# First loads by single k-tiles, small parameters behind them, h transposed before its modulation, raw weights in idle attention tiles

## The chip, the cores and the metric

The kernel runs on one core of one Trainium2 chip. The metric is the device time of one execution in microseconds (us), the median of several; lower is better. The core has five engines that run side by side: TensorE (PE, matmuls and transposes), VectorE (DVE), ScalarE (ACT), GpSimd (POOL) and SyncE (SP, which here only issues DMAs). Data go from HBM to SBUF by DMA, and matmuls write to PSUM, of which the kernel uses eight banks of 128 x 512 floats.

## The reference

Two layers; 256 tokens, width 1024. All values are float32.

```python
def hybrid_layer(x, c, ...):
    mod = silu(c) @ w_ada + b_ada                       # 1024 x 3072
    shift, scale, gate = split(mod, 3)
    h = rms_norm(x, norm_g) * (1 + scale) + shift
    z = h @ w_in                                        # 1024 x 2976
    c_q, c_kv, k_rope, g_mla, q_b, k_b, v_b, g_moba = split(z)
    o_mla = mla_attention(c_q, c_kv, k_rope, positions, ...)
    o_moba = moba_attention(q_b, k_b, v_b, ...)
    y = concat([silu(g_mla) * o_mla, silu(g_moba) * o_moba]) @ w_out
    return x + gate * y
```

With 256 tokens MoBA has a single block, so both attentions are causal attentions with 8 heads, MLA with low-rank q and kv (`w_uq`, `w_ukv`) and rotary keys, MoBA with a relative bias.

## The kernel before

**Precision by splitting.** A weight piece is 256 rows of a weight matrix (two k-tiles of 128) by up to 512 columns, loaded raw as float32. ACT (or DVE) casts it to a rounded high part `whi`, DVE subtracts to get the low part `wlo`, and h is split in the same way. Each product is three matmuls: high by high, high by low, low by high. `plan` lists the pieces in the order of their use: for layer 0 first a, ga, gb for each pair of k-tiles (pieces 0 to 11), then uq, uq, ukv, bq, bk, bv and the output weights. `load_piece` (L540) loads one into a buffer, `splitter` and `split_lo` (L553, L574) split it, the first `HALVES` pieces by single k-tiles.

**The first stage of layer 0.** `w_ada` for shift (w=0) and scale (w=1) is loaded in five rounds of k-tiles (0), (1), (2, 3), (4, 5), (6, 7) by `load_first` (L1315), into tiles that attention needs only later. `sum_first` (L1331) sums each round on PE with silu(c), copies the sums out, transposes them and makes shift and gain of these k-tiles. `first_h` (L1418) and `h_T` (L783) transpose the normalised x, apply gain and shift in PSUM and write h high and low. Then the projections a (tile za), ga (zga) and gb (zgb) run k-tile by k-tile. `loader` (L1427) sets the order of these loads on SP's queue. Sixteen small parameters are loaded from POOL's queue right at the start.

**Behind it** come bq, MLA's q and kv, bk, bv, attention in eight steps, and the output projection y; layer 1 does the same with its own order. `modulation` (L718) loads layer 0's gate and layer 1's shift and scale in blocks of 512 columns and sums each on PE in a gap.

**What sets the order.** Instructions are emitted by a planner at build time. `Clock` (L75) keeps an estimated time for each engine and for the DMA queue (D); generators yield the time or the condition for which they wait, and what is ready by the estimate comes first. `run` (L164) goes through the projections' units, and lets optional work in (`offer`) where PE would wait. The engines execute what was emitted for them in order and wait on semaphores. Numbers such as `SLACK`, `BIAS`, `AHEAD`, `URGENT` and `D_0` change only that order. Until the estimate reaches `DUMMY`, `warm_up` (L1436) puts filler matmuls (tile `warm`) into PE's queue.

Of the kernel before, what the change touches and what calls it, by code (L numbers as in the profile page):

```python
# [11 lines left out]
F32 = mybir.dt.float32  # L12
# [9 lines left out]
D = 1024  # L22
# [9 lines left out]
RAW = 3  # L32
ADA_LAG = 0.25
# [4 lines left out]
DENSE = 0.6  # L38
BQ_FIRST = 2
ON = ("T", "T")  # L40
EARLY = True
FIRST = 0
# [12 lines left out]
AHEAD = 4  # L55
SLACK = 0.35
URGENT = 2
BIAS = 0.7
WARM = 7
D_LAT = 0.95  # L60
D_0 = 4.0
HALVES = 12
# [157 lines left out]
class Metered:  # L220
# [18 lines left out]
    def _cost1(self, op, out, args, kw):  # L239
        if op == "preload_act_table_set":  # L240
            return 1.3
        n = 1
        for d in out.shape[1:]:
            n *= d
        if self._name == "P":
            return 0.06 + n / 510.0
        if self._name == "T":
            lhs = kw["lhsT"] if "lhsT" in kw else args[1]
            mode = lhs.shape[0] <= 64, out.shape[0] if out.shape[0] in (32, 64) else 128
            switch = 0.16 if mode != self.__dict__.get("_mode", mode) else 0.0  # L250
            self._mode = mode
            if "lhsT" not in kw:
                return switch + 0.109
            if lhs.dtype != F32:
                return switch + 0.012 + n / 2400.0
            return switch + {32: 0.01 + n / 2400.0, 64: 0.01 + n / 1200.0}.get(out.shape[0], max(0.218, n / 600.0))
        aps = sum(not isinstance(v, (int, float, str)) for k, v in kw.items() if k in ("scale", "bias"))
        ins = [a for a in list(args[1:]) + [kw.get("in0"), kw.get("in1")] if hasattr(a, "space")]
        psum = PSUM in [a.space for a in ins]
        if self._name == "A":  # L260
            return (0.061 if psum else 0.096) + n / 1200.0 + 0.093 * aps + (0.19 if "accum_out" in kw else 0.0)
        if op == "tensor_reduce":
# [9 lines left out]
def trunk(ctx, tc, x, c, positions, norm_g, w_ada, b_ada, w_in, mla_q_norm_g, mla_w_uq,  # L272
# [32 lines left out]
    nc.sync.dma_start(xs[:, 0], x[0, 0:128, :])  # L305
    nc.sync.dma_start(xs[:, 1], x[0, 128:256, :])
# [7 lines left out]
    G.dma_start(pos_i, positions[0].rearrange("(t p) -> t p", p=128))  # L314
    G.dma_start(flat[:, 0:16], invf.unsqueeze(0))
# [11 lines left out]
    G.dma_start(rows_b[V_QN:V_QN + 4], mla_q_norm_g.rearrange("l (k p) -> (l k) p", p=128))  # L327
    G.dma_start(rows_b[V_KN:V_KN + 2], mla_kv_norm_g)
    G.dma_start(rows_b[V_MQ:V_MQ + 2, 0:64], mla_q_g[:, 0:64])
    G.dma_start(rows_b[V_MK:V_MK + 2, 0:64], mla_k_g[:, 0:64])  # L330
    for i, g in enumerate((mla_q_g, mla_k_g)):
        for l in range(DEPTH):
            c0 = 16 + 32 * (DEPTH * i + l)
            G.dma_start(flat[:, c0:c0 + 32], g[l:l + 1, 64:96])
    for a in (0, 64):
        G.dma_start(rows_b[V_BQ:V_BQ + 2, a:a + 64], moba_q_g)
        G.dma_start(rows_b[V_BK:V_BK + 2, a:a + 64], moba_k_g)
# [4 lines left out]
    G.dma_start(rb_s[0:32], rel_bias)  # L342
    oh_s = sp.tile([33, 384], F32, tag="PT", bufs=PTS, name="oh_s")
    G.dma_start(oh_s, onehot)
# [3 lines left out]
                    base=128, channel_multiplier=1)  # L348

# [162 lines left out]
    def load(dst, src, *keys):  # L512
        nc.sync.dma_start(dst, src)
        n = 128 * 4
        for d in dst.shape[1:]:
            n *= d
        clk.t["D"] = max(clk.t["D"], clk.now + 1.7) + 0.05 + n / (3.6e5 if dst.shape[-1] >= 256 else 2.5e5)
        clk.mark(*keys, at=clk.t["D"] + D_LAT)
# [19 lines left out]
    early = ("raw", "raw", "raw", "ga_hi", "ga_lo", "gate", "vb", "raw", "raw", "raw", "ga_hi", "ga_lo")  # L538

    def load_piece(i):  # L540
        key, a, src = pieces[i]
        tag = early[i] if i < len(early) else "raw"
        yield from take(tag)
        pool_ = {"raw": wp, "vb": sp}.get(tag, cp)
        raw = pool_.tile([128, 2, 512], F32, tag=tag, bufs=RAW if tag == "raw" else 1, name=f"raw_{key[0]}{key[1]}_{a}")
        load(raw[:, :, 0:src.shape[2]], src, ("raw", i))
        halves[key, a] = raw, tag

# [4 lines left out]
    def splitter():  # L553
        for i, (key, a, src) in enumerate(pieces):
            n = src.shape[2]
            yield from until(("raw", i))
# [7 lines left out]
            halves[key, a] = hi, lo  # L564
            for ks in parts(i):
                yield from clk.idle("A", urgent, lambda: held(i))
                copy(hi[:, ks, 0:n], raw[:, ks, 0:n])
            start(split_lo(i, raw, tag), clk.end + clk.LAT)
# [5 lines left out]
    def split_lo(i, raw, tag):  # L574
        key, a, src = pieces[i]
        n = src.shape[2]
        hi, lo = halves[key, a]
        for ks in parts(i):
            yield from clk.idle("V", lambda: i <= used[0] + URGENT, lambda: held(i))
            V.tensor_tensor(lo[:, ks, 0:n], raw[:, ks, 0:n], hi[:, ks, 0:n].bitcast(F32), op=ALU.subtract)  # L580
        give(tag)
        clk.mark(("w", key, a))
# [84 lines left out]
    def on_vector(todo, begin, period):  # L667

        for i, ((m, w, j), k) in enumerate(todo):
# [15 lines left out]
            if k == KT - 2:  # L685
                yield
                start(gate_sums(m, j, acc, ones), clk.now)
# [30 lines left out]
    def modulation(l, period):  # L718

        by_k = lambda blocks: [(b, k) for b in blocks for k in range(0, KT, 2)]  # L720
        gates_ = by_k((l, 2, j) for j in range(2))
        next_ = by_k((l + 1, w, j) for j in range(2) for w in (1, 0)) if l + 1 < DEPTH else []
        start(ada_loader(l, (gates_ + next_)))
        if ON[l] == "V":
            yield clk.now + period[1]
            start(on_vector(gates_, clk.now, period[0]), clk.now)
        start(on_tensor((gates_ if ON[l] == "T" else []) + next_, clk.now + period[1], period[2]), clk.now)
# [102 lines left out]
    def proj_unit(name, l, o, k, t):  # L830
# [11 lines left out]
        return unit((("w", key, k // 2), ("h", l, k, t)), k == 0, emit, key, k // 2)  # L842

    def gate_unit(name, l, o, k, b):
# [14 lines left out]
        return unit((("w", key, k // 2), ("h", l, k, 0), ("h", l, k, 1)), k == 0, emit, key, k // 2)  # L859


    def layer(l):
# [86 lines left out]
        def mla_q(t):  # L949
# [8 lines left out]
            for g in range(2):  # L958
                yield from take("ps")
# [28 lines left out]
        def mla_kv(t):  # L988
# [10 lines left out]
            for g in range(2):  # L999
                yield from take("ps")  # L1000
# [426 lines left out]
    def loader():  # L1427
        order = [(0, 1), (0, 0), 0, (1, 1), (1, 0), 1, 2, (2, 1), (2, 0), 3, 4, (3, 1), (3, 0), 5, 6, (4, 1), (4, 0),
                 *range(7, len(pieces))]
        for what in order:  # L1430
            if isinstance(what, int):
                yield from load_piece(what)
            else:
                yield from load_first(*what)
# [26 lines left out]
    clk.mark(("x", 0), at=4.6)  # L1461
    clk.mark(("x", 1), at=6.2)
# [3 lines left out]
    start(angles(), 30)  # L1466
    start(vectors(), 6.2)
    start(loader(), 0.0)
    for r in range(len(rounds)):
        start(sum_first(r))  # L1470
# [68 lines left out]
```

## Time and profile before

| | |
|---|---|
| time, median of 3 runs | 310.87 us (310.55 to 311.05) |
| the profiled execution, in all | 309.71 us |
| its span | 307.6 us |
| PE busy | 296.6 us (96%) |
| DVE busy | 217.0 us (71%) |
| ACT busy | 211.0 us (69%) |
| POOL busy | 13.6 us (4%) |
| DMA | 65.2 MB, 212 GB/s in the mean |

The span runs from the first to the last instruction of the profile; the time in all has some 2 us more around it. Busy shares are means over stages with different limits. Matmul ends are modelled and overlap with the next matmul, so a busy PE can still lose time between two kinds of matmul. A row "31.89 0.69 DVE L230 ..." starts at 31.89 us and lasts 0.69; L230 is the line through which all metered engines' instructions are issued, so instructions are told apart by their tiles: `out<-in`.

### The profile page before, as it was taken

The numbers are of one execution on the slowest core, as the hardware profiler recorded it, in microseconds if no ns is written. First come the engines' busy times: TensorE is split into PE (matmuls) and PEld (weight loads), VectorE is DVE, ScalarE is ACT, GpSimd is POOL, SyncE is SP. The second block draws the span as 40 slices with busy tenths as digits, with TensorE's granted clock in tenths as the row PEclk, the third lists the DMA queues.
The fourth block names the chain that finished last, engine by engine and source line by source line (L and its number), as shares of the span: only waits on it lengthen the run. The fifth ranks groups of instructions, "written<-read, shape, count | busy, mean of one in ns | idle before, by whom it ended". The sixth has DMA issues, their size and how long they took to land.

```text
span 307.6 us, 5595 instructions
## 1 busy us (share of the span) xinstructions
PE 296.6 (96%) x1976; PEld 234.7 (76%) x1976; DVE 217.0 (71%) x635; ACT 211.0 (69%) x516; POOL 13.6 (4%) x40
## 2 busy tenths in 40 slices
PE   6989999999999899999999998999999999999995
PEld 5757779986668588665775968879999778777884
DVE  1344798664997979784876778699877598857544
ACT  5443367796695886986678896877587959685710
POOL 8700000000010000000000000000000000000000
PEclk9799999999999999999999999999999999999998
DMA  7999996895979975781843976665606450621012
GB/s 237 315 351 355 362 372 193 275 389 204 359 212 376 329 256 172 255 286 25 320 120 122 336 258 215 200 168 175 205 12 208 128 174 32 207 78 57 3 65 71
DMA packets 40299, 65.20 MB, mean 212 GB/s; under 512 B 2685, under 2 KB 16325, under 8 KB 40272
## 3 DMA queue, kind: packets, MB, share of 16 engines
q1 hardware_dynamic: 39360, 63.71, 62.5%
q0 software_dynamic: 816, 1.12, 1.4%
q8 instruction: 15, 0.25, 0.3%
q14 instruction: 12, 0.10, 0.1%
q10 hardware_dynamic: 96, 0.02, 0.0%
HBM read 63.79 MB, written 1.06 MB: 211 GB/s over the span
## 4 chain that ended last, share of the span: by engine, by line
PE 81%; DVE 7%; DMA 5%; ACT 5%; issue 1%; SPq 0%
PE y L230 15%; PE zbv L230 7%; PE ada L230 7%; PE zgb L230 7%; PE zga L230 7%; PE zbq L230 6%; PE zbk L230 6%; PE s L230 6%; PE za L230 4%; PE oT L230 4%; DMA raw_bv<-in_w_in_dram 3%; PE ptr L230 3%; PE q L230 2%; PE qtr L230 2%; DMA ada<-in_w_ada_dram 2%; PE warm L230 1%
## 5 line engine op out<-in xcount | busy, mean ns | idle before, releaser
L230 ACT ACTIVATE P<-P,sm 128x128 f32<-128x128 f32 (+1 forms) x116 | 47.8, 446 | 6.7 <-DVE sm L230 6.6
L230 PE MATMUL ada<-ada,crep 128*32 128x512 f32 (+2 forms) x272 | 25.2, 471 | 1.5 <-DMA ada<-in_w_ada_dram 1.5
L230 PE MATMUL y<-whi_o,gm 128*128 128x512 f32 (+1 forms) x72 | 23.8, 386 | 0.5 <-DVE gm L230 0.5
L230 DVE TENSOR_TENSOR wlo_o<-raw_o,whi_o 128x1024 fp32r<-128x1024 f32 x16 | 19.5, 1222 | 3.8 <-ACT whi_o L230 3.8
L230 PE MATMUL zga<-h_hi,whi_ga 128*128 128x256 f32 x64 | 19.3, 302 | 0.0
L230 PE MATMUL zgb<-h_hi,whi_gb 128*128 128x256 f32 x64 | 19.2, 300 | 0.0
L230 PE MATMUL zga<-h_hi,wlo_ga 128*128 128x256 f32 x64 | 18.2, 285 | 0.7 <-DVE wlo_ga L230 0.7
L230 PE MATMUL zgb<-h_hi,wlo_gb 128*128 128x256 f32 x64 | 18.1, 283 | 0.0
L230 PE MATMUL zga<-h_lo,whi_ga 128*128 128x256 f32 x64 | 18.1, 283 | 0.0
L230 PE MATMUL zgb<-h_lo,whi_gb 128*128 128x256 f32 x64 | 18.1, 283 | 0.0
L230 ACT CAST whi_o<-raw_o 128x1024 fp32r<-128x1024 f32 x15 | 15.6, 1044 | 1.6 <-PE y L230 1.6
L230 PEld LDWEIGHTS y<-whi_o,gm 128*128 128x128 f32 x72 | 13.1, 189 | 3.4 <-DVE gm L230 0.9
L230 PE MATMUL ptr<-ident,P 128*128 128x128 f32 x96 | 15.6, 273 | 0.0
L230 ACT ACTIVATE htr<-htr,ss 128x128 f32<-128x128 f32 (+1 forms) x21 | 9.7, 473 | 8.4 <-PE htr L230 5.0
L230 PEld LDWEIGHTS ptr<-ident,P 128*128 128x128 f32 x96 | 12.1, 140 | 4.4 <-DVE sm L230 0.8
L230 PEld LDWEIGHTS ada<-ada,crep 128*32 128x32 f32 x272 | 6.4, 110 | 11.4 <-issue 8.8
L230 PE MATMUL y<-whi_o,ga_hi 128*128 128x512 f32 (+1 forms) x36 | 15.0, 417 | 0.0
L230 PE MATMUL zbv<-whi_bv,h_hi 128*128 128x512 f32 x32 | 14.3, 446 | 0.0
L230 DVE CUSTOM_DVE_ANT_0 P<-s,bt 128x128 f32<-128x128 f32 (+1 forms) x32 | 9.5, 354 | 6.7 <-PE s L230 6.6
L230 PE MATMUL y<-whi_o,ga_lo 128*128 128x512 f32 (+1 forms) x36 | 13.4, 373 | 0.5 <-DVE ga_lo L230 0.5
L230 PE MATMUL zbk<-whi_bk,h_hi 128*128 128x512 f32 x32 | 13.8, 431 | 0.0
L230 PEld LDWEIGHTS zgb<-h_hi,whi_gb 128*128 128x128 f32 x64 | 12.2, 191 | 2.1 <-issue 2.1
(336 smaller groups left out, 878.5 us busy)
## 6 DMA issues: line engine op xcount, KB each, us to landing
ada<-in_w_ada_dram SPq DMA_DIRECT2D x44, 512.0 KB, 7.8
raw_o<-in_w_out_dram SPq DMA_DIRECT2D x16, 512.0 KB, 3.7
raw_ga<-in_w_in_dram SPq DMA_DIRECT2D x8, 512.0 KB, 6.0
raw_gb<-in_w_in_dram SPq DMA_DIRECT2D x8, 512.0 KB, 6.1
raw_bq<-in_w_in_dram SPq DMA_DIRECT2D x8, 512.0 KB, 3.9
raw_bk<-in_w_in_dram SPq DMA_DIRECT2D x8, 512.0 KB, 4.5
raw_bv<-in_w_in_dram SPq DMA_DIRECT2D x8, 512.0 KB, 4.7
raw_a<-in_w_in_dram SPq DMA_DIRECT2D x8, 416.0 KB, 6.1
```

The source lines that it names most:

```text
L230: r = f(*args, **kw)
```

## The change

- **Loads.** x, then round 0 of `w_ada`, then one k-tile each of pieces 0, 1 and 2 (a, ga, gb), round 1, the other k-tile of each, round 2 and so on as before. The three pieces are loaded by two DMAs each. A k-tile of a piece can be used when that k-tile is split.
- **Small parameters.** The 16 small loads leave POOL's queue at the start and are issued behind a copy that waits for the last load of round 0.
- **h.** For layer 0, `h_T` transposes the normalised x without waiting for shift and gain; these are applied in PSUM as before, once they are there.
- **Raw weights.** Four instead of three raw buffers; pieces 12 to 19 go to `bqT`, `bkT`, `kT`, raw, raw, raw, `ga_hi`, `ga_lo`.
- **Planner.** New numbers and estimates, another order of the `w_ada` blocks behind the first stage, one spare PSUM bank asked for by MLA's q and kv.

```diff
-RAW = 3
-ADA_LAG = 0.25
+RAW = 4
+ADA_LAG = 0.1
-DENSE = 0.6
+DENSE = 0.3
-ON = ("T", "T")
+ON = ("TTTTTT", "TT")
+LOADS = ("x0", "x1", (0, 1), (0, 0))
+LATER = True
+SINGLE = 3
+BEHIND = ("bqT", "bkT", "kT", "raw", "raw", "raw", "ga_hi", "ga_lo")
+QS = 1
+ANGLES = 30
+AFTER_0 = (0, 1, 2)
+AFTER_1 = (0, 1, 2)
-FIRST = 0
+ORDER = (0, 4, 1, 2, 5, 3)
+FIRST = 8
-AHEAD = 4
-SLACK = 0.35
-URGENT = 2
-BIAS = 0.7
+AHEAD = 3
+SLACK = 0.25
+URGENT = 1
+BIAS = 0.65
-D_0 = 4.0
-HALVES = 12
+D_0 = 2.1
+HALVES = 9
...
+            if mode[0]:
+                return switch + max(0.109, n / 1200.0)
...
-    nc.sync.dma_start(xs[:, 0], x[0, 0:128, :])
-    nc.sync.dma_start(xs[:, 1], x[0, 128:256, :])
...
-    G.dma_start(pos_i, positions[0].rearrange("(t p) -> t p", p=128))
-    G.dma_start(flat[:, 0:16], invf.unsqueeze(0))
...
-    G.dma_start(rows_b[V_QN:V_QN + 4], mla_q_norm_g.rearrange("l (k p) -> (l k) p", p=128))
...
+    behind = cp.tile([128, 1], F32, name="behind")
+
+    def small_loads():
+
+        if LATER:
+            yield from until(("first", 0, 0, 1))
+            G.tensor_copy(behind, st[0, 0][-1][:, 0:1])
+        G.dma_start(pos_i, positions[0].rearrange("(t p) -> t p", p=128))
+        G.dma_start(flat[:, 0:16], invf.unsqueeze(0))
+        G.dma_start(rows_b[V_QN:V_QN + 4], mla_q_norm_g.rearrange("l (k p) -> (l k) p", p=128))
...
+        G.dma_start(rb_s[0:32], rel_bias)
+        G.dma_start(oh_s, onehot)
+        return
+        yield
...
-        clk.t["D"] = max(clk.t["D"], clk.now + 1.7) + 0.05 + n / (3.6e5 if dst.shape[-1] >= 256 else 2.5e5)
+        clk.t["D"] = max(clk.t["D"], clk.now + 1.7) + 0.02 + n / (3.6e5 if dst.shape[-1] >= 256 else 2.9e5)
...
-    early = ("raw", "raw", "raw", "ga_hi", "ga_lo", "gate", "vb", "raw", "raw", "raw", "ga_hi", "ga_lo")
+    early = ("raw", "raw", "raw", "ga_hi", "ga_lo", "gate", "vb", "raw", "raw", "raw", "ga_hi", "ga_lo", *BEHIND)
 
     def load_piece(i):
         key, a, src = pieces[i]
         tag = early[i] if i < len(early) else "raw"
         yield from take(tag)
-        pool_ = {"raw": wp, "vb": sp}.get(tag, cp)
+        pool_ = {"raw": wp, "ga_hi": cp, "ga_lo": cp, "gate": cp}.get(tag, sp)
         raw = pool_.tile([128, 2, 512], F32, tag=tag, bufs=RAW if tag == "raw" else 1, name=f"raw_{key[0]}{key[1]}_{a}")
-        load(raw[:, :, 0:src.shape[2]], src, ("raw", i))
         halves[key, a] = raw, tag
+        if i < SINGLE:
+            for k in range(2):
+                load(raw[:, k:k + 1, 0:src.shape[2]], src[:, k:k + 1], ("raw", i, k))
+                yield
+        else:
+            load(raw[:, :, 0:src.shape[2]], src, ("raw", i, 0), ("raw", i, 1))
 
 
     def held(i):
@@ -553,7 +577,7 @@
     def splitter():
         for i, (key, a, src) in enumerate(pieces):
             n = src.shape[2]
-            yield from until(("raw", i))
+            yield from until(("raw", i, 0))
             if i > used[0] + AHEAD:
                 yield lambda: i <= used[0] + AHEAD
             yield from take("w")
@@ -562,10 +586,12 @@
             nm = f"{key[0]}{key[1]}_{a}"
             hi, lo = (wp.tile([128, 2, 512], F32R, tag=t_, bufs=SPLITS, name=f"{t_}_{nm}") for t_ in ("whi", "wlo"))
             halves[key, a] = hi, lo
+            start(split_lo(i, raw, tag), clk.now)
             for ks in parts(i):
+                yield from until(("raw", i, ks.start))
                 yield from clk.idle("A", urgent, lambda: held(i))
                 copy(hi[:, ks, 0:n], raw[:, ks, 0:n])
-            start(split_lo(i, raw, tag), clk.end + clk.LAT)
+                clk.mark(("hi", i, ks.start))
             yield
 
     def parts(i):
@@ -576,8 +602,10 @@
         n = src.shape[2]
         hi, lo = halves[key, a]
         for ks in parts(i):
+            yield from until(("hi", i, ks.start))
             yield from clk.idle("V", lambda: i <= used[0] + URGENT, lambda: held(i))
             V.tensor_tensor(lo[:, ks, 0:n], raw[:, ks, 0:n], hi[:, ks, 0:n].bitcast(F32), op=ALU.subtract)
+            clk.mark(*(("w", key, a, k) for k in ((0, 1) if ks.stop - ks.start == 2 else (ks.start,))))
         give(tag)
...
-        gates_ = by_k((l, 2, j) for j in range(2))
-        next_ = by_k((l + 1, w, j) for j in range(2) for w in (1, 0)) if l + 1 < DEPTH else []
-        start(ada_loader(l, (gates_ + next_)))
-        if ON[l] == "V":
-            yield clk.now + period[1]
-            start(on_vector(gates_, clk.now, period[0]), clk.now)
-        start(on_tensor((gates_ if ON[l] == "T" else []) + next_, clk.now + period[1], period[2]), clk.now)
+        blocks = [(l, 2, j) for j in range(2)]
+        if l + 1 < DEPTH:
+            n_ = [(l + 1, w, j) for j in range(2) for w in (1, 0)]
+            blocks = [(n_ + blocks)[i] for i in ORDER]
+        of = lambda e: by_k(b for b, on in zip(blocks, ON[l]) if on == e)
+        start(ada_loader(l, by_k(blocks)))
+        start(on_vector(of("V"), clk.now, period[0]), clk.now)
+        start(on_tensor(of("T"), clk.now + period[1], period[2]), clk.now)
...
-        return unit((("w", key, k // 2), ("h", l, k, t)), k == 0, emit, key, k // 2)
+        return unit((("w", key, k // 2, k % 2), ("h", l, k, t)), k == 0, emit, key, k // 2)
...
-                yield from take("ps")
+                yield from take("ps", spare=QS)
...
-        order = [(0, 1), (0, 0), 0, (1, 1), (1, 0), 1, 2, (2, 1), (2, 0), 3, 4, (3, 1), (3, 0), 5, 6, (4, 1), (4, 0),
+        single = {i: load_piece(i) for i in range(SINGLE)}
+        order = [*LOADS, *AFTER_0, (1, 1), (1, 0), *AFTER_1, (2, 1), (2, 0), 3, 4, (3, 1), (3, 0), 5, 6, (4, 1), (4, 0),
                  *range(7, len(pieces))]
         for what in order:
-            if isinstance(what, int):
+            if what in ("x0", "x1"):
+                t = int(what[1])
+                load(xs[:, t], x[0, tok(t), :], ("x", t))
+            elif isinstance(what, int) and what < SINGLE:
+                for y_ in single[what]:
+                    if y_ is None:
+                        break
+                    yield y_
+            elif isinstance(what, int):
                 yield from load_piece(what)
             else:
...
-    clk.mark(("x", 0), at=4.6)
-    clk.mark(("x", 1), at=6.2)
...
-    start(angles(), 30)
+    start(angles(), ANGLES)
     start(vectors(), 6.2)
     start(loader(), 0.0)
+    start(small_loads(), 0.0)
```

## Rows read from the trace of the kernel before

**Rows 1.** Busy time by stretch: stretch, length, PE PEld DVE ACT POOL, PEclk, DMA share, GB/s
```profile
0.00:15.70 15.70, 12.65 (x105) 9.79 (x105) 4.15 (x17) 7.93 (x18) 12.18 (x38) 0.89 0.96 278
...
20.00:32.40 12.40, 12.34 (x116) 8.69 (x116) 6.14 (x14) 4.07 (x9) 0.00 (x0) 1.00 1.08 356
...
32.40:62.80 30.40, 30.15 (x234) 27.40 (x231) 24.52 (x71) 19.89 (x43) 0.00 (x0) 1.00 0.89 299
...
100.00:200.00 100.00, 97.23 (x609) 72.40 (x608) 76.07 (x233) 79.30 (x217) 0.00 (x0) 1.00 0.66 223
```

**Rows 2.** Timeline of PE, 9 to 20 us: start, us, instruction, idle before it
```profile
9.72 1.23 PE L230 MATMUL warm<-ident 128*128 128x128 f32 x4
...
10.88 0.66 PE L230 MATMUL ada<-ada,crep 128*32 128x128 f32 x8
...
15.68 0.46 PE L230 MATMUL za<-whi_a,h_hi 128*128 128x416 f32 x1 [0.23 <-ACT h_hi L230]
...
19.77 0.38 PE L230 MATMUL zga<-h_hi,wlo_ga 128*128 128x256 f32 x1 [0.75 <-DVE wlo_ga L230]
```

**Rows 3.** Timeline of PE, 100 to 200 us: the two longest waits
```profile
105.97 0.66 PE L230 MATMUL ada<-ident,ev 128*128 128x128 f32 x4 [0.84 <-ACT ev L230]
...
185.89 0.46 PE L230 MATMUL za<-whi_a,h_lo 128*128 128x416 f32 x1 [0.95 <-DVE h_lo L230]
```

**Rows 4.** Loads of tile ada: the last of round 0, then of round 2
```profile
L513 SPq DMA_DIRECT2D ada<-in_w_ada_dram x1: 368/368/368, 4.6 to 4.6; - x1
...
DMA to landing us min/median/max: 5.0/5.0/5.0
...
L513 SPq DMA_DIRECT2D ada<-in_w_ada_dram x1: 1761/1761/1761, 14.0 to 14.0; - x1
...
DMA to landing us min/median/max: 10.7/10.7/10.7
```

**Rows 5.** Busy time by stretch, one microsecond each
```profile
5.00:6.00 1.00, 0.87 (x6) 0.68 (x4) 0.00 (x0) 0.99 (x5) 0.81 (x2) 1.00 1.00 314
...
11.00:12.00 1.00, 1.00 (x10) 0.62 (x11) 0.00 (x0) 0.40 (x2) 0.53 (x1) 0.50 1.23 286
```

**Rows 6.** Chain of work that ended last: start, us, what
```profile
51.56 2.88 PE zgb L230 x24
...
93.47 9.98 DMA raw_bv<-in_w_in_dram
...
111.86 2.76 PE zbv L230 x12
```

**Rows 7.** Timeline of PE, ACT and DVE, 24.9 to 33 us: round 2
```profile
24.99 0.64 PE L230 MATMUL ada<-ada,crep 128*32 128x256 f32 x8
...
25.70 0.59 ACT L230 COPY ev<-ada 128x512 f32<-128x512 f32 x1 [4.83 <-PE ada L230]
...
26.80 0.60 PE L230 MATMUL ada<-ident,ev 128*128 128x128 f32 x4
...
28.17 0.16 DVE L230 SCALAR_TENSOR_TENSOR ss<-ss,vec_a 128x2 f32<-128x2 f32 x1
...
29.92 0.64 PE L230 MATMUL ada<-ada,crep 128*32 128x256 f32 x8
...
30.03 1.11 ACT L230 ACTIVATE htr<-htr,ss 128x256 f32<-128x256 f32 x2 [1.63 <-PE htr L230]
...
31.40 1.07 PE L230 MATMUL ada<-ada,crep 128*32 128x256 f32 x16
...
31.89 0.69 DVE L230 TENSOR_TENSOR h_lo<-htr,h_hi 128x512 fp32r<-128x512 f32 x1
...
32.40 0.46 PE L230 MATMUL za<-whi_a,h_hi 128*128 128x416 f32 x1
```

**Rows 8.** Groups of instructions, 80 to 180 us: splits of one weight piece
```profile
L230 DVE TENSOR_TENSOR wlo_bv<-raw_bv,whi_bv 128x1024 fp32r<-128x1024 f32 x4 | 4.9, 1222 | 1.3 <-ACT whi_bv L230 1.3
...
L230 ACT CAST whi_bv<-raw_bv 128x1024 fp32r<-128x1024 f32 x4 | 4.2, 1045 | 3.0 <-DMA raw_bv<-in_w_in_dram 3.0
```

More of the change, by code (lines that the diff above doesn't have):

```diff
@@ L326, in trunk @@
     G.memset(rows_b, 1.0)
-    G.dma_start(rows_b[V_QN:V_QN + 4], mla_q_norm_g.rearrange("l (k p) -> (l k) p", p=128))
[L328 to L337, printed above, removed]
     ones = cp.tile([128, 128], F32, name="ones")
@@ L341, in trunk @@
     G.memset(rb_s, NEG)
-    G.dma_start(rb_s[0:32], rel_bias)
     oh_s = sp.tile([33, 384], F32, tag="PT", bufs=PTS, name="oh_s")
-    G.dma_start(oh_s, onehot)
     cmask = cp.tile([128, S], F32, name="cmask")
@@ L348, in trunk @@
                     base=128, channel_multiplier=1)
+    behind = cp.tile([128, 1], F32, name="behind")
[6 more added lines that the diff above has]
+        G.dma_start(rows_b[V_QN:V_QN + 4], mla_q_norm_g.rearrange("l (k p) -> (l k) p", p=128))
+        G.dma_start(rows_b[V_KN:V_KN + 2], mla_kv_norm_g)
+        G.dma_start(rows_b[V_MQ:V_MQ + 2, 0:64], mla_q_g[:, 0:64])
+        G.dma_start(rows_b[V_MK:V_MK + 2, 0:64], mla_k_g[:, 0:64])
+        for i, g in enumerate((mla_q_g, mla_k_g)):
+            for l in range(DEPTH):
+                c0 = 16 + 32 * (DEPTH * i + l)
+                G.dma_start(flat[:, c0:c0 + 32], g[l:l + 1, 64:96])
+        for a in (0, 64):
+            G.dma_start(rows_b[V_BQ:V_BQ + 2, a:a + 64], moba_q_g)
+            G.dma_start(rows_b[V_BK:V_BK + 2, a:a + 64], moba_k_g)
+        G.dma_start(rb_s[0:32], rel_bias)
+        G.dma_start(oh_s, onehot)
+        return
+        yield
     ct_ps = bank("ct_ps")
@@ L686, in on_vector, with acc_sums @@
                 yield
-                start(gate_sums(m, j, acc, ones), clk.now)
+                start(gate_sums(m, j, acc, ones) if w == 2 else
+                      acc_sums(m, w, tuple(range(4 * j, 4 * j + 4)), acc), clk.now)
+    def acc_sums(l, w, ks, acc):
+        yield from until("vec_a")
+        yield from take("ps")
+        p_ = bank(f"ada{l}{w}{ks[0]}")
+        for b in range(4):
+            T.matmul(p_[:, b:b + 1], lhsT=acc[:, b * 128:b * 128 + 128], rhs=ones[:, 0:1], start=True, stop=True)
+        give("acc")
+        yield
+        ss_finish(l, w, ks, p_[:, 0:4])
+        give("ps")
     def gate_rows(l, j, p_):
@@ L858, in emit @@
                 clk.mark((name, l, b))
-        return unit((("w", key, k // 2), ("h", l, k, 0), ("h", l, k, 1)), k == 0, emit, key, k // 2)
+        return unit((("w", key, k // 2, k % 2), ("h", l, k, 0), ("h", l, k, 1)), k == 0, emit, key, k // 2)
     def layer(l):
@@ L999, in mla_kv @@
             for g in range(2):
-                yield from take("ps")
+                yield from take("ps", spare=QS)
                 o = bank(f"kv{l}{t}{g}")
```

## The prediction

> **What bounds the kernel now.** I read the busy time by stretch first [rows 1]. TensorE (PE) is the only engine that is nearly full: of the 30.4 us from 32.4 to 62.8 it is busy for 30.15, and of the 12.4 us before that for 12.34. So from 20 us on, a microsecond is won only where PE gets its work sooner or has less of it. Two places are left. In the first 15.7 us PE is busy for 12.65 us, but mostly with fillers and small sums: the first projection matmul starts at 15.68 [rows 2]. And between 100 and 200 us PE idles 2.77 us [rows 1], in four waits, the longest of them 0.95 and 0.84 us [rows 3]. The next thing to see is that the DMA engines are full as well (a share of 1.08 from 20 to 32.4 and 0.89 in the 30 us behind it [rows 1]), so the early gain is limited by when bytes land, not only by PE.
>
> The chain to the first projection, in the timeline of PE [rows 2]: the fourth load of round 0 of `w_ada` is issued at 4.6 us and lands 5.0 us later, at 9.6 [rows 4]. PE sums it at 10.88 only, since it stands behind four filler records that start at 9.72 and take 1.23 us [rows 2], in a stretch with a granted clock of 0.50, the 1.2 GHz level [rows 5]. Copy, transposes, gain and h follow, with more fillers and the transposes of x between them, and za starts at 15.68. The gate projections of k 0 still wait for w_low of ga, until 19.77 [rows 2].
>
> **Part 1, order of the first loads, and single k-tiles.** Before, round 0 is followed by both k-tiles of piece a (0.43 MB), then round 1 (1.05 MB), then ga and gb (0.52 MB each). After, one k-tile each of a, ga and gb (0.74 MB) stands before round 1 and the other one behind it. Everything that k 0 needs then stands in the first 2.84 MB, where it was 4.6 MB; the bytes up to the end of round 2 are the same 6.7 MB. The chain for round 0, from the landing at 9.6: sums 0.4, copy, transposes, three small DVE steps and modulation 2.0, h_hi 0.4, hand-overs 0.5: za at about 13 instead of 15.7, and the gate matmuls of k 0 (24 of them, 2.9 us by the chain's 2.88 for as many [rows 6]) directly behind it. So PE is through with k 0 and k 1 several microseconds sooner than before, where round 3's sums at 31.40 follow them directly [rows 7].
>
> This doesn't go through to the end, because k 2 and 3 need round 2, whose last load lands at 14.0 + 10.7 = 24.7 us [rows 4]; no byte in front of it has gone. Its chain in the trace [rows 7]: last sums at 24.99, the gain finished at 28.33, the modulation at 30.03 for 1.11 us, h_lo done at 32.58, and za of k 2 at 32.40: 7.6 us from sums to h, and PE right behind it. Hence what counts is by how much that chain shortens.
>
> **Part 2, h transposed unmodulated** (FIRST 0 to 8). Before, `h_T` transposes x only when the gain is known: gain done at 28.33, modulation only at 30.03, because the transposes stand in PE's queue behind k 1's matmuls and ACT waits 1.63 us for them [rows 7]. After, they are done beforehand and the modulation can start right behind the gain: 1.6 us less. That costs no work, four transposes are only moved, and one PSUM bank is held longer. PE is also less full at that time, so the transposes of the sums don't wait behind k 1 (0.4 us). From the durations of these rows, sums 0.6, copy 0.6, transposes 0.6, three small DVE steps 0.6, modulation 1.1, h_hi 0.7, h_lo 0.7 and some 0.7 of hand-overs make 5.6 instead of 7.6 us. Lower bound of the shortening: nothing, if ACT or DVE is busy with weight splits just then; upper bound 2.5.
>
> **Part 3, small parameters later.** 16 small POOL loads leave the first 15 us. With only round 0 in flight the DMA moves 314 GB/s, with the small loads beside round 1 it moves 286 [rows 5]. That is at most 9% over some 8 us, 0.7 us; I take 0.4, since only part of the stretch runs at the lower rate. On POOL's queue a copy now waits for the landing of round 0, and all 16 loads stand behind it, until about 20 us. Their first user is `angles`, which the planner starts at 30 us (L1466), so the cover is 10 us; without it DVE would wait on POOL's loads and the weight splits behind it on DVE with it.
>
> **Sum for the first stage.** za of k 2 comes 2.0 + 0.4 + 0.6 (h_hi is enough to start, h_lo follows) = 3.0 us sooner, at 29.4. But 24 records of round 3's sums, 0.64 + 1.07 = 1.7 us, were done before 32.4 in the old order [rows 7]; at 29.4 their data has hardly landed, so they now lie behind. PE being full from there on, 3.0 - 1.7 = 1.3 us remain; I take **1.4**, with 0.4 (round 2 only 0.4 earlier, the chain as long as before) and 3.0 (the sums find a hole) as the ends. The PE clock can change little here: should it be granted at the 1.2 GHz level again for 3 us, 1.5 us of matmul time are lost before round 2, where PE has to wait anyway.
>
> What a split load costs: the trace has loads of 256 KB with 512-byte rows, which move 314 GB/s [rows 5], and a stretch of 512 KB loads at 356 [rows 1]; the single k-tiles have 208 or 256 KB and rows of 1.7 or 2 KB, a form that no row has. If they ran as the former, their 1.47 MB would take 4.7 instead of 4.1 us, round 2 would land 0.6 later, and the stage would gain 0.8. I take the latter, since the queue holds other loads all the time, and keep 0.8 in the range. The Trainium skill (DMA: Bandwidth & Descriptors, Rules for kernel authors) speaks against this part: for the highest bandwidth it wants at least 1 MiB in one DMA, which would make the sum 0.8 rather than 1.4; no row here shows either.
>
> **Part 4, more places for raw weights** (RAW 4, idle attention tiles for pieces 12 to 19). The chain goes through a load of raw_bv for 9.98 us [rows 6], and PE waits 0.84 us for a copy on ACT [rows 3], which in the chain stands behind the split of that piece. With a fourth buffer and free tiles the loads after 45 us are issued earlier, and this wait should go: 0.8 us. The other three waits are for h_lo and for the attention output; nothing in the change is aimed at them. So 0.8, between 0 and 2.77.
>
> **Part 5, planner numbers and modulation order.** Lookahead 4 to 3, urgency 2 to 1, BIAS, SLACK, HALVES, QS and the order of the `w_ada` blocks only reorder instructions. The last block of layer 1's gain keeps its last place and gate 1 moves from second to fifth of six, which costs something only if the residual that reads it comes sooner. The density of fillers (0.6 to 0.3) counts for nothing: PE's rows have no tile `idle`. I take zero, with the price of the wrong side in rival D.
>
> **Forecast.** The profiled execution has a span of 307.6 and takes 309.71 in all; 307.6 - 1.4 - 0.8 = 305.4 span, 307.5 in all. Its time is 1.16 under the median of 310.87, so against the median: 310.87 - 2.2 = **308.7 us**.
>
> **Rivals.**
> A is the forecast: 308.7, its own range 307.4 to 310.2. Chance 0.45.
> B, everything goes through: the first stage gives 3.0 and all four waits go (2.8): 305.1. For it: the waits are short and separate, and a better order can hide each. Against: three of them are dependences of attention that stay. Chance 0.23.
> C, round 2 holds the stage: its landing doesn't move, since the single loads cost the rate that the small ones give back, ACT and DVE splits fill the place of the transposes, and the waits at 105 to 186 only move. Gain 0.4, 310.5, give or take 0.5. So the change does what it says at k 0 and k 1, and PE waits longer before k 2. Chance 0.16. (The rule of the Trainium skill named above speaks for it.)
> D, slower: weight splits come just too late. A piece needs 1.05 us on ACT and 1.22 on DVE [rows 8], 2.5 with hand-overs, while PE uses a piece of twelve matmuls up in 2.76 us [rows 6]. With urgency at one piece ahead only 0.3 us of slack is left when ACT or DVE is late, and both are busy for 76 to 79 of the 100 us from 100 on [rows 1]. Sixteen pieces of that size pass between 80 and 180 us (bk 4, bv 4, o 8). From a mean lateness of 0.14 us (2.2 / 16) on, the gain is gone; at 0.25 us it costs 4.0: 312.7. Against it: a lookahead of three pieces gives 8 us if the engines find idle time. Chance 0.16.
>
> **How the numbers follow.** A difference under 0.2% (0.6 us) can't be told from no change here. Faster by more than that: A almost whole, B, a third of C: 0.72. Same: most of C, edges of A and D: 0.13. Slower: D and a little of C: 0.15. The range goes down to B's 305.1 (half of B lies below: 0.11) and up to 311.8 (some two thirds of D lie above: 0.09).
>
> **What would show it.** Right: the first za near 13 us and the gates of k 0 without a break behind it; za of k 2 at about 29.5 with an idle PE of 1 to 2 us ahead of it; the first zbq about 1.4 us before 62.8; modulation of round 2 within 0.2 us of the gain; the wait at 105.97 gone. Wrong: za of k 2 later than 31.5 (C), PE waits for wlo or whi tiles between 80 and 180 summing to over 2 us (D), or PE idle under 1 us from 100 to 200 and zbq before 60.5 (B). The prediction fails altogether if PE's work between 63 and 300 us itself gets shorter or longer by the new order, by fewer or more switches between kinds of matmul, which no idle time shows.

## The result, and the profile after

The kernel after takes **307.39 us** (median of 5 executions, 307.21 to 307.44), the kernel before beside it 310.98 (310.55 to 313.11). The ratio is 0.9886, with a 95% interval of 0.9856 to 0.9915. That is 1.3 us under the forecast of 308.7 and inside the range. The profiled execution has a span of 305.3 us (before: 307.6), so the traces have to explain 2.3 us. The other 1.3 of the 3.6 between the medians are not in them: the profiled execution of before lies under its own median.

Busy time by stretch, kernel after (columns as in [rows 1]):

```profile
0.00:15.70 15.70, 12.57 (x104) 9.32 (x105) 4.24 (x16) 7.49 (x17) 7.48 (x31) 1.00 0.94 279
20.00:32.40 12.40, 11.57 (x103) 7.79 (x95) 4.67 (x12) 4.57 (x9) 0.53 (x1) 1.00 1.09 352
32.40:62.80 30.40, 30.40 (x238) 27.23 (x239) 23.67 (x65) 19.52 (x42) 0.00 (x0) 1.00 1.06 377
100.00:200.00 100.00, 99.94 (x623) 74.58 (x623) 76.03 (x232) 75.82 (x214) 0.00 (x0) 1.00 0.68 225
```

Against [rows 1]: PE's idle time from 100 to 200 us has fallen from 2.77 to 0.06, and the DMA share from 32.4 to 62.8 has risen from 0.89 to 1.06, since the weights behind the first stage are now fetched there. The start is less changed. The granted clock is 1.00 in the first 15.7 us instead of 0.89, and PE idles 0.83 us between 20 and 32.4 where it idled 0.06.

The same columns for two long stretches, first from the first matmul of bq (tile zbq, 62.6 us before and 62.1 after) to the first projection of layer 1 (tile za), then from there to the end of the last y. Before:

```profile
62.60:173.10 110.50, 108.68 (x664) 78.21 (x663) 83.38 (x267) 84.53 (x214) 1.46 (x2) 1.00 0.72 249
173.10:304.00 130.90, 129.95 (x847) 108.71 (x845) 96.37 (x263) 92.31 (x230) 0.00 (x0) 1.00 0.44 138
```

After:

```profile
62.10:170.30 108.20, 108.14 (x663) 78.14 (x662) 85.32 (x270) 83.14 (x213) 1.47 (x2) 1.00 0.70 237
170.30:301.40 131.10, 131.09 (x861) 110.44 (x859) 92.83 (x257) 95.39 (x233) 0.00 (x0) 1.00 0.43 136
```

So the gain lies almost whole in one place. The first stage ends 0.5 us sooner, the **middle stretch** is 2.3 us shorter, layer 1 is 0.2 longer, and what follows the last y is 0.3 longer (3.6 and 3.9 us): 2.3 in all. In the middle stretch of before PE idles 1.82 us (110.50 - 108.68): the 0.84 at 105.97 of [rows 3], and two waits that the prediction set aside. PE's timeline of before:

```profile
132.69 0.50 PE L230 MATMUL y<-whi_o,ga_lo 128*128 128x512 f32 x1 [0.52 <-DVE ga_lo L230]
...
169.09 0.50 PE L230 MATMUL y<-whi_o,gm 128*128 128x512 f32 x1 [0.46 <-DVE gm L230]
```

After, all three are gone. In layer 1 the 0.95 at 185.89 [rows 3] is gone as well, but nothing is won by it: the 14 records by which that stretch has grown are fillers, put where the wait was. PE's timeline of after:

```profile
181.62 1.72 PE L239 MATMUL idle<-ident 128*128 128x128 f32 x14
183.10 0.43 PE L239 MATMUL za<-whi_a,h_hi 128*128 128x416 f32 x1
```

**The first stage after.** PE's timeline, 12 to 32 us, answering [rows 2] and [rows 7]:

```profile
12.94 0.43 PE L239 MATMUL ada<-ada,crep 128*32 128x128 f32 x8 [0.72 <-DMA ada<-in_w_ada_dram]
13.83 0.43 PE L239 MATMUL ada<-ada,crep 128*32 128x128 f32 x8 [0.46 <-DMA ada<-in_w_ada_dram]
...
14.38 0.44 PE L239 MATMUL za<-whi_a,h_hi 128*128 128x416 f32 x1
...
17.70 0.38 PE L239 MATMUL zga<-h_hi,whi_ga 128*128 128x256 f32 x1
...
27.48 0.66 PE L239 MATMUL ada<-ident,ev 128*128 128x128 f32 x4 [0.83 <-ACT ev L239]
...
30.97 0.64 PE L239 MATMUL ada<-ada,crep 128*32 128x256 f32 x8
31.54 0.46 PE L239 MATMUL za<-whi_a,h_hi 128*128 128x416 f32 x1
```

ACT's timeline of the same time:

```profile
16.32 0.54 ACT L239 CAST whi_a<-raw_a 128x416 fp32r<-128x416 f32 x1 [2.62 <-DMA raw_a<-in_w_in_dram]
...
17.03 1.14 ACT L239 CAST whi_ga<-raw_ga 128x512 fp32r<-128x512 f32 x2
...
25.96 0.98 ACT L239 CAST whi_a<-raw_a 128x416 fp32r<-128x416 f32 x2 [5.62 <-DMA raw_a<-in_w_in_dram]
26.85 0.58 ACT L239 COPY ev<-ada 128x512 f32<-128x512 f32 x1
...
29.25 1.11 ACT L239 ACTIVATE htr<-htr,ss 128x256 f32<-128x256 f32 x2 [0.71 <-DVE ss L239]
30.39 0.59 ACT L239 CAST h_hi<-htr 128x512 fp32r<-128x512 f32 x1
```

and the last step of the gain on DVE:

```profile
29.05 0.16 DVE L239 SCALAR_TENSOR_TENSOR ss<-ss,vec_a 128x2 f32<-128x2 f32 x1
```

Two engines stand still behind work whose data is late. PE waits at 12.94 and 13.83 for round 1, which stands in its queue ahead of za, so za starts at 14.38 and not near 13. ACT waits 2.62 us for the second k-tile of a, and only then casts the first of ga, so the gates of k 0 start at 17.70. And the copy of round 2's sums (the last of them start at 24.55) stands behind a cast of raw_a that has waited 5.62 us for its load; PE waits 0.83 us for that copy. The modulation at 29.25 follows the gain directly, as forecast, but the time won there is lost ahead of it. Nor does za of k 2 wait for that chain at the end: h_hi is done at 30.98, and PE is busy, last with round 3's sums at 30.97, until za starts at 31.54.

### The profile page after: what moved, and what is told of

It reads as the page before. It is cut to its first block, busy times and chain, and to the rows that moved or that the text cites. A ratio compares the mean times of both kernels' runs of the same rounds, so it can differ in the third digit from the quotient of the medians.

```text
span 305.3 us, 5609 instructions
## 1 busy us (share of the span) xinstructions
PE 296.6 (97%) x1984; PEld 234.7 (77%) x1984; DVE 214.4 (70%) x628; ACT 212.9 (70%) x517; POOL 13.0 (4%) x41
## 3 DMA queue, kind: packets, MB, share of 16 engines
q1 hardware_dynamic: 39408, 63.71, 62.8%
HBM read 63.79 MB, written 1.06 MB: 212 GB/s over the span
## 4 chain that ended last, share of the span: by engine, by line
PE 89%; DMA 7%; SPq 1%; DVE 1%; ACT 0%; issue 0%; DVEq 0%
PE y L239 15%; PE ada L239 8%; PE zbv L239 8%; PE zbk L239 7%; PE zgb L239 7%; PE zbq L239 7%; PE zga L239 7%; PE s L239 6%; PE za L239 5%; PE oT L239 4%; DMA ada<-in_w_ada_dram 4%; PE ptr L239 4%; DMA raw_a<-in_w_in_dram 3%; PE q L239 3%; PE qtr L239 2%; PE kv L239 2%
## 5 line engine op out<-in xcount | busy, mean ns | idle before, releaser
L239 PE MATMUL ptr<-ident,P 128*128 128x128 f32 x96 | 15.7, 274 | 0.0
L239 DVE TENSOR_TENSOR oT<-oT,sg 128x256 f32<-128x256 f32 x16 | 6.9, 429 | 12.5 <-ACT whi_bv L239 7.3
L239 DVE TENSOR_TENSOR wlo_a<-raw_a,whi_a 128x416 fp32r<-128x416 f32 (+1 forms) x11 | 8.6, 786 | 9.8 <-ACT whi_a L239 9.8
L239 ACT CAST whi_a<-raw_a 128x416 fp32r<-128x416 f32 (+1 forms) x11 | 7.5, 696 | 9.6 <-DMA raw_a<-in_w_in_dram 8.8
```

The lines of the kernel that those rows point to most:

```text
L239: r = f(*args, **kw)
```

## The experiments

Each kernel is the kernel after with some of its settings changed; "numbers" below are the planner's. All were timed against the kernel before in the same session.

**1. Each part undone.** Raw places as before:

```diff
-RAW = 4
-BEHIND = ("bqT", "bkT", "kT", "raw", "raw", "raw", "ga_hi", "ga_lo")
+RAW = 3
+BEHIND = ()
```

> The changed kernel with three raw buffers and without the idle attention tiles for weights (pieces 12 and later all in raw); all else as changed. Theory M (most of the gain lies between 62 and 173 us, and the extra places for raw weights bring most of that): 309.0 to 310.0, the PE waits between 100 and 173 us come back to 1 us or more, first zbq still near 62.2. Theory S (the first stage brings the gain): within 0.5 of 307.4. Theory P (the planner's numbers bring it): within 0.5 of 307.4.

Measured: 312.48 us (311.22 to 313.56), ratio 1.0046 [1.0025, 1.0067]. The middle stretch is 112.7 us, with 4.16 us of idle PE, and the whole gain is gone. Theory M has the place right, but its time is 2.5 us short.

The planner's numbers as before (here several to a line):

```diff
-ADA_LAG, DENSE, AHEAD, SLACK, URGENT, BIAS = 0.1, 0.3, 3, 0.25, 1, 0.65
-ORDER, HALVES, QS = (0, 4, 1, 2, 5, 3), 9, 1
+ADA_LAG, DENSE, AHEAD, SLACK, URGENT, BIAS = 0.25, 0.6, 4, 0.35, 2, 0.7
+ORDER, HALVES, QS = (4, 5, 0, 1, 2, 3), 12, 0
```

> The changed kernel with the planner's numbers of before (lookahead 4, slack 0.35, urgency 2, bias 0.7, 12 pieces split by halves, no spare bank, filler density 0.6, lag 0.25, gate blocks first). Theory P: 310 or more, waits between 100 and 173 us as before. Theory M: 307.9 to 308.6. Theory S: within 0.5 of 307.4.

Measured: 315.89 us (315.66 to 316.15), ratio 1.0162 [1.0139, 1.0185]. "Zero" for the numbers was badly wrong: with the rest of the change in place they are worth 8.5 us. The trace has 66 filler matmuls, in runs of 2.62 and 5.07 us, and layer 1 takes 135.6 us instead of 131.1.

h transposed only when the gain is known (`FIRST = 0`):

> The changed kernel with x transposed for layer 0 only when shift and gain are known, as before. Theory S: 308.5 or more, since round 2's h comes 1 to 1.6 us later and PE waits for it. Theory M: 307.5 to 308.1, since za of k 2 is held by the copy that stands behind the cast of a late raw_a on ACT as well.

Measured: 309.16 us (309.00 to 310.10), ratio 0.9958 [0.9934, 0.9983]. The first zbq comes at 62.7, 0.6 us later than after; the middle stretch has 1.35 us of idle PE again.

Load order and single k-tiles undone (`SINGLE = 0`, `AFTER_0 = (0,)`, `AFTER_1 = (1, 2)`):

> The changed kernel with the old order of the first loads: round 0, both k-tiles of a, round 1, ga and gb whole. Theory S: 308.8, the 1.4 us that were forecast come from it. Theory M: 307.4 to 308.0, since ga's first cast stands behind the second k-tile of a on ACT in the changed kernel, so the single k-tiles of ga and gb are not used early, and za of k 2 stays near 31.5.

Measured: 309.12 us (309.10 to 309.15), ratio 0.9944 [0.9923, 0.9965]. The first zbq comes at 63.2, and 0.79 us of idle PE are back in the middle stretch.

What follows: undone one at a time, the parts cost 5.1, 8.5, 1.8 and 1.7 us, 17 in all, of a change that gained 3.6. They don't add. (The late small loads were not undone alone.) No theory holds throughout: M's times were too short in all four, P's bound held for the numbers, and S's times (308.5 or more, and 308.8) fit the last two. By place, the raw places lose in the middle stretch, the numbers there and in layer 1, the early transposes mostly in the middle stretch, and the load order about half there and half (1.1 us) before the first zbq. Each edit makes the planner lay the whole program out anew, and waits come back far behind the edit.

**2. What holds the first stage.** The cast of piece 3 waits, in the plan, for the copy of round 2's sums:

```diff
+        clk.mark(("ev", r))
...
+            if i == 3:
+                yield from until(("ev", 2))
```

> The changed kernel, but piece 3 (raw_a of k 2 and 3) is cast only behind the copy of round 2's sums on ACT, so that the copy doesn't wait for that load. Theory H: copy at 25.2 instead of 26.85, za of k 2 at about 30 instead of 31.5, time 306.0 to 306.9. Theory W: no change, within 0.4 of 307.4.

Measured: 307.36 us (307.12 to 307.95), ratio 0.9894 [0.9872, 0.9916], the same as after. ACT's timeline of this kernel:

```profile
27.16 0.59 ACT L239 COPY ev<-ada 128x512 f32<-128x512 f32 x1 [4.90 <-PE ada L239]
27.65 0.98 ACT L239 CAST whi_a<-raw_a 128x416 fp32r<-128x416 f32 x2
...
29.83 1.11 ACT L239 ACTIVATE htr<-htr,ss 128x256 f32<-128x256 f32 x2 [0.16 <-DVE ss L239]
```

The copy now stands first, and the chain from the last sums (26.46) to za of k 2 (32.41) is 5.95 us, where after has 24.55 to 31.54, 7.0. In this execution the first matmuls ran slowly (last section) and za of k 0 started only at 16.21, 1.8 us later than after; the first zbq came at 62.7, 0.6 later. This profiled execution is the slowest of the four (307.95); the other three (307.12 to 307.40) are no faster than after's. So a chain 1 us shorter brought nothing that the times show, which speaks for W and against H. Since the three have no profile, how their start went stays open.

Splits of the first three pieces independent of each other, so that the first k-tile of ga doesn't stand behind the second of a:

```diff
+            g = split_hi(i, raw, hi, n)
+            if i < SINGLE:
+                start(g, clk.now)
+            else:
+                yield from g
```

> The changed kernel, but the first three pieces are split independently, so that the casts of ga's and gb's first k-tile don't stand behind that of a's second one on ACT. If round 2 holds the stage (theory H: za of k 2 waits for the chain of round 2, whose copy stands behind the cast of a late raw_a on ACT): gates of k 0 from about 15 instead of 17.7 us, za of k 2 still at 31 to 31.6, time within 0.5 of 307.4. If PE's work is what holds the stage (theory W): everything 1.5 to 2.5 us sooner, about 305.5.

Measured: 309.70 us (309.46 to 310.67), ratio 0.9962 [0.9939, 0.9985], 2.3 slower than after, a time that neither theory had. The gates of k 0 do start at 16.9 instead of 17.7, directly behind za. The copy of round 2's sums finds ACT free, and h_hi of k 2 is done at 29.62, 1.4 us sooner than after. But za of k 2 starts at 31.38 all the same, because round 3's sums stand ahead of it in PE's queue and wait for their load. ACT's timeline of this kernel, then PE's:

```profile
25.25 0.59 ACT L239 COPY ev<-ada 128x512 f32<-128x512 f32 x1 [5.44 <-PE ada L239]
...
29.03 0.59 ACT L239 CAST h_hi<-htr 128x512 fp32r<-128x512 f32 x1
```

```profile
30.40 0.64 PE L239 MATMUL ada<-ada,crep 128*32 128x256 f32 x8 [0.78 <-DMA ada<-in_w_ada_dram]
30.97 0.66 PE L239 MATMUL htr<-ident,xr 128*128 128x128 f32 x4
31.38 0.43 PE L239 MATMUL za<-whi_a,h_hi 128*128 128x416 f32 x1
```

So here neither the chain of round 2 nor PE's own work alone sets za of k 2, but the order of PE's queue and the landing of round 3. The first zbq is at 63.1, a microsecond later than after, with a wait of 1.27 us for h_hi at 54.29, and 0.9 us of idle PE are back in the middle stretch. Mending the start locally made the plan worse further on.

**3. The fillers of after** (`DENSE = 0.0`):

> The changed kernel without the 14 filler records (1.5 us) at 181.6 us in layer 1. If they only fill a wait for h_lo (theory F): PE idles 1.0 to 1.3 us there and the time stays within 0.3 of 307.4. If they stand in front of work that could run (rival): 0.4 to 1.0 us faster, 306.4 to 307.0.

Measured: 307.24 us (307.04 to 307.83), ratio 0.9891 [0.9865, 0.9916], the same as after. PE's timeline of this kernel:

```profile
183.40 0.46 PE L239 MATMUL za<-whi_a,h_lo 128*128 128x416 f32 x1 [1.09 <-DVE h_lo L239]
```

The wait for h_lo is back, 1.09 us, and layer 1 takes 130.9 us instead of 131.1. Theory F holds: after's fillers fill a wait and cost at most 0.3 us; that this wait "went" is an appearance.

**4. The change cut into three parts, alone and in pairs.** Loading (load order, single k-tiles, late small loads, early transposes), raw places, and numbers. The settings of each part are the ones shown above, with `LATER = False` for the loading.

Numbers alone:

> Only the planner's side of the change: its new numbers, estimates and block order, with the old load order, the small loads early, x transposed late and three raw buffers without extra tiles. Theory P (the numbers alone bring the gain): 308 or less. Theory M (the numbers need the extra places for raw weights; with three buffers they lose): 311.5 to 313.5.

Measured: 310.19 us (309.42 to 312.77), ratio 0.9978 [0.9951, 1.0004]. This lies between the two theories' ranges.

Loading alone:

> The loading side of the change alone (load order, single k-tiles, small loads later, h transposed early); raw places and planner numbers as before (no fillers are asked for beyond the old density 0.6). So far: planner numbers alone 310.2, loading with numbers 312.5, loading with places 315.9, all three 307.4. Theory A (each part has a price of its own and they add): loading is worth 312.5 - 310.2 = +2.3, so 313.3, with the stretch from the first zbq to the first za of layer 1 at 112 us or more. Theory I (the parts have no price of their own, every edit makes another order of the whole stretch behind the first stage): first zbq within 0.7 of 62.1, and the time set by how long PE waits between 62 and 170 us, which may be anything from 0 to 4 us: 309 to 314, not told by the sum.

Measured: 322.24 us (320.76 to 323.04), ratio 1.0355 [1.0304, 1.0406]. Neither theory had such a time in its range.

Raw places alone:

> The raw places alone (fourth buffer, idle attention tiles), loading and planner numbers as before. Theory A (parts add): 311.0 + 4.9 - 2.3 = 313.6, as loading with places was 4.9 over before and loading 2.3. Theory M of mine (places take the waits of the stretch from 62 to 170 us away whatever the rest): that stretch falls from 110.5 to 108.2 to 108.7 and the time is 308.7 to 309.3. Theory I (an order planned anew by numbers that were not chosen for it): the stretch stays at 109.5 or more and the time is 310 to 316.

Measured: 315.06 us (314.83 to 316.01), ratio 1.0139 [1.0087, 1.0192]. My theory M, that places clear the middle stretch whatever the rest, falls; time and stretch (112.0) are those of theory I.

Places and numbers, without the loading:

> Raw places and planner numbers, without the loading side. Theory M (places with their numbers clear the stretch from 62 to 170 us): stretch 108.2 to 108.7, first zbq at 61.7 as with the numbers alone, so 307.0 to 307.6, as fast as the whole change: the loading order would be worth nothing. Theory S (the loading is worth something at the start): first zbq at 62.6 or later, 308.0 to 309.0. Theory I: the stretch is 109.2 or longer with one or more waits of 0.5 to 1 us, 308.5 to 310.

Measured: **307.05 us** (306.44 to 307.50), ratio 0.9871 [0.9828, 0.9914]. Theory M in its narrower form holds: time and middle stretch (108.2) are in its ranges, and the first zbq comes at 61.4. Beside places and numbers the loading side of the change is worth nothing. The 1.8 and 1.7 us that two pieces of it cost when they were undone singly were the price of another plan.

The old numbers with loading and places, without fillers:

> Loading and places with the old planner numbers as in the run that took 315.9, but no filler matmuls at all (density 0). There the trace had 66 filler records and PE busy for 5.3 us more than in the kernel after. Theory F (the fillers themselves push the work back): 310 to 311.5, last y end some 5 us sooner. Theory W (the fillers only fill a wait, as they did in the kernel after): 315 to 316, and PE idle instead, some 5 us between 165 and 195 us.

Measured: 313.45 us (313.10 to 314.19), ratio 1.0087 [1.0059, 1.0114], halfway between the theories. Fillers cost 2.4 of the 8.5 us.

All in one table (us; "middle" from the first zbq to the first za of layer 1, "idle" PE's idle time in it, "layer 1" from there to the end of the last y; a part that is in is marked +):

| loading | places | numbers | time | first zbq | middle | idle | layer 1 |
|---|---|---|---|---|---|---|---|
| before | | | 310.98 | 62.6 | 110.5 | 1.8 | 130.9 |
| | | + | 310.19 | 61.7 | 112.0 | 3.6 | 130.7 |
| | + | | 315.06 | 61.5 | 112.0 | 1.7 | 135.6 |
| | + | + | 307.05 | 61.4 | 108.2 | 0.1 | 131.1 |
| + | | | 322.24 | 62.2 | 115.8 | 5.1 | 136.8 |
| + | | + | 312.48 | 62.0 | 112.7 | 4.2 | 130.7 |
| + | + | | 315.89 | 62.6 | 112.0 | 1.6 | 135.6 |
| + | + | + | 307.39 | 62.1 | 108.2 | 0.1 | 131.1 |
| + | + | +, no fillers | 307.24 | 62.3 | 108.2 | 0.1 | 130.9 |
| + | + | no fillers | 313.45 | 62.0 | 110.9 | 2.5 | 134.4 |

(Only the row "before" has the old code. All others keep the new estimates of when loads land, x's loads issued by the planner, a piece used by single k-tiles, and the earlier start of `split_lo`. With the old numbers, loading alone, places alone and both together have 44, 66 and 66 fillers, which count as busy.)

In the kernels without fillers there, the middle stretch is PE's work of 108.1 to 108.7 us plus its waits. Places **and** numbers take the waits away, and for the wait that was longest in before the path can be read. The loads and splits of tile bv in the kernel with numbers alone (count, duration in ns, first to last start in us):

```profile
L532 SPq DMA_DIRECT2D raw_bv<-in_w_in_dram x8: 367/368/519, 80.8 to 243.3; - x8
...
L239 ACT CAST whi_bv<-raw_bv x3: 1048/1053/1057, 87.8 to 102.2; 128x1024 fp32r<-128x1024 f32 x3
```

its ACT:

```profile
102.21 1.06 ACT L239 CAST whi_bv<-raw_bv 128x1024 fp32r<-128x1024 f32 x1
...
103.61 0.57 ACT L239 COPY ev<-ada 128x512 f32<-128x512 f32 x1
```

and its PE:

```profile
104.23 0.66 PE L239 MATMUL ada<-ident,ev 128*128 128x128 f32 x4 [1.03 <-ACT ev L239]
105.42 1.16 PE L239 MATMUL s<-kT,qT 96*128 96x128 f32 x8 [0.53 <-ACT PT L239]
108.70 0.64 PE L239 MATMUL qtr<-ident,kn 128*96 128x128 f32 x4 [0.96 <-DVE kn L239]
```

With places and numbers:

```profile
L532 SPq DMA_DIRECT2D raw_bv<-in_w_in_dram x8: 367/368/368, 66.7 to 235.9; - x8
...
L239 ACT CAST whi_bv<-raw_bv x4: 1041/1050/1056, 81.6 to 90.9; 128x1024 fp32r<-128x1024 f32 x4
```

Without places the first load of bv is issued at 80.8 (before: 83.3) and the last cast starts at 102.2 (before: 103.5), on ACT with two short steps between it and the copy for which PE then waits 1.03 us; the next wait, 0.53, is for ACT as well. What holds the third, 0.96 for DVE, was not followed. With places the load goes out at 66.7, the last cast starts at 90.9, and there is no cast on ACT between 98 and 112 us to wait behind. The fourth buffer and the attention tiles were not tried apart.

Without the new numbers the places do harm in layer 1. With places alone, the two long stretches and PE's timeline at 184 us:

```profile
61.50:173.50 112.00, 110.35 (x685) 80.99 (x685) 83.41 (x264) 82.26 (x212) 1.47 (x2) 1.00 0.72 244
173.50:309.10 135.60, 134.87 (x891) 113.75 (x889) 93.88 (x258) 96.07 (x237) 0.00 (x0) 1.00 0.40 127
```

```profile
184.58 5.07 PE L239 MATMUL idle<-ident 128*128 128x128 f32 x44
```

44 fillers, 5.07 us in all, stand ahead of a za for which before waited 0.95. Without fillers the same settings show how much of that is a real wait. PE's waits from the first za of layer 1 on, old numbers without fillers (us in total, times, longest):

```profile
PE qtr L239 <- DVE qn L239: 1.8, 1, 1.8
PE za L239 <- DVE h_lo L239: 1.4, 1, 1.4
PE ada L239 <- ACT evg L239: 0.7, 1, 0.7
```

There layer 1 takes 134.4 us, with 3.9 us of idle PE. Which single number brings these waits was not tried.

## Why the prediction was right, and where its steps were not

The sign and the size held, and of the six signs named for "right" two came: the modulation directly behind the gain, and the wait at 105.97 gone. za of k 0, the gates of k 0, za of k 2 and the first zbq came later than forecast. The sum held by luck, since two errors cancelled: 1.4 + 0.8 was forecast, the traces have 0.5 + 2.3, less 0.5 behind. And the 0.5 can't be put down to the loading, since with places and numbers alone the first zbq is sooner still.

- **Part 1, order of the first loads.** Wrong step: "za at about 13 ... and the gate matmuls of k 0 directly behind it". It followed the data of round 0 and not the queues: PE had round 1's sums ahead of za, ACT the second k-tile of a ahead of ga. za came at 14.38, the gates at 17.70. The table goes further: the four pairs with and without loading are 307.05 and 307.39, 310.19 and 312.48, 315.06 and 315.89, and (with the reservation above) 310.98 and 322.24. Loading never helped, and in the three pairs that differ in nothing else the first zbq is 0.3 to 1.1 us later with it. Without the loading za of k 0 comes as early as after, and the gates sooner. PE's timeline with places and numbers:

```profile
14.28 0.46 PE L239 MATMUL za<-whi_a,h_hi 128*128 128x416 f32 x1
...
16.91 0.39 PE L239 MATMUL zga<-h_hi,whi_ga 128*128 128x256 f32 x1 [0.46 <-ACT whi_ga L239]
```

What moved the first zbq from 62.6 to between 61.4 and 61.7 without the loading stays open. All these kernels share the code named below the table. The start of the profiled execution of before is another candidate: its matmuls ran slowly from 9 to 12 us, and the only other trace with a slow start (last section) has za of k 0 at 16.21 and its first zbq at 62.7.
- **The price of split loads.** Taken at nothing, rightly: the first 15.7 us move 279 GB/s and 20 to 32.4 us 352. With the load order and the single k-tiles undone, all else as after, it is 278 and 351. The Trainium skill (DMA: Bandwidth & Descriptors, Rules for kernel authors), cited in the prediction, wants at least 1 MiB in one DMA for the highest bandwidth, and loads of 208 to 256 KB are further from it than the whole pieces. These traces show no loss by that, with other loads in flight all the time.
- **Part 2, early transposes.** Right in its mechanism (modulation at 29.25, directly behind a gain whose last step starts at 29.05), mis-sized in its result: the 1.63 us of [rows 7] went, but the copy ahead of it came behind a late cast, so from the last sums to za it takes 7.0 us (to the end of h_lo 7.15, where 5.6 was forecast). The lower bound "nothing, if ACT is busy with weight splits just then" was the case, and it should have been the value, since before already had a cast next to that copy. za of k 2 came at 31.54, at the sign for rival C (31.5); for the first stage C was the better forecast. A second step failed: that round 3's sums "now lie behind". 16 of the 24 still stood ahead of za in PE's queue, and where the chain did come out as short as forecast (experiment 2, h_hi done at 29.62), za still started only at 31.38.
- **Part 3, small loads.** 0.4 was taken; no rate shows it. The reading behind it was wrong: at 5 us in before, two small loads had been issued already, and the row at 314 GB/s is not one of round 0 alone. After, with none of the 16 issued before 10 us, the same stretch is no faster (before: 314, then 327):

```profile
5.00:6.00 1.00, 1.00 (x6) 0.77 (x4) 0.00 (x0) 1.00 (x4) 0.00 (x0) 1.00 0.95 309
6.00:7.00 1.00, 0.77 (x4) 0.62 (x3) 0.00 (x0) 1.00 (x5) 0.00 (x0) 1.00 1.00 296
```

With places and numbers but the small loads still at the start, the first 15.7 us move 278 GB/s, as with them moved (279).
- **Part 4, raw places.** Right as to the place and its mechanism: the wait at 105.97 is gone, because bv is loaded 16 us and split 12 us earlier (first load at 67.3, last cast at 91.6). Wrong step: "the other three waits ...; nothing in the change is aimed at them. So 0.8". The 0.52 and 0.46 us in the same stretch went too. The whole stretch was rearranged, and the right count was all of its 1.82 us; the remaining 0.5 is less busy time (108.68 to 108.14 with one record less), whose cause was not found.
- **Part 5, numbers.** "I take zero" is the worst term. They are worth 8.5 us beside loading and places, 8.0 beside the places alone, 9.8 beside the loading alone, and 0.8 by themselves (against before), with an interval that takes in nothing. "The density of fillers counts for nothing" was right for this kernel by luck (0.3 at most) and wrong for its neighbours: 2.4.
- **The rivals.** B asked for an idle PE under 1 us from 100 to 200 and a first zbq before 60.5: the first came (0.06), the second didn't (62.1). D's wait is in no trace: between 80 and 180 us PE waits for no wlo or whi tile after, nor in any of the kernels with the old numbers, whose waits are for other tiles.

## What to carry to other kernels

When a program's order is planned by estimates, an edit is a new order of everything behind it: take all waits of the fullest engine in a stretch as the range, and test parts in combination, since here one part alone, beside the new estimates, lost 11 us where the whole gained 3.6. An earlier load is worth only what the in-order queues between it and the full engine let through: list what stands ahead of each step on its engine and when that work's own data lands. A wait that turns into fillers has not gone, so compare the length of the stretch, not the idle time.

## What was not expected of the hardware

Before, the granted clock falls to 0.50 (the 1.2 GHz level) between 9 and 12 us [rows 5]; ahead of it PE had waited 1.45 us for a load, until 7.32, and it came back while PE was busy without a break. PE's timeline of before:

```profile
7.32 0.43 PE L230 MATMUL ada<-ada,crep 128*32 128x128 f32 x8 [1.45 <-DMA ada<-in_w_ada_dram]
```

After, the wait for that load is 0.28 us and the clock stays at 1.00, through the gaps of 0.72 and 0.46 us before za as well. In the profiled execution of experiment 2's first kernel, whose start was slow, the durations show it and the clock column doesn't. Its PE, then one microsecond of it by stretch:

```profile
10.94 0.66 PE L239 MATMUL ada<-ada,crep 128*32 128x128 f32 x8
```

```profile
10.00:11.00 1.00, 1.00 (x14) 0.57 (x10) 0.29 (x1) 0.54 (x1) 1.00 (x3) 1.00 1.04 367
```

Eight such matmuls take 0.66 us here, as they do in before at 10.88 [rows 2] in a stretch with a granted clock of 0.50, and 0.43 in after at 12.94; yet the column says 1.00. So the duration of a known group should be looked at beside the column. za was 1.8 us later than after, the end of the stage 0.6. That kernel's edit shortens a chain in the stage, so what the slow start alone cost is not shown.
